# A two-model kernel on one core: shared banks for the output product, rope partners by DMA, a norm by pairs of tiles, and more convolution taps per portion

## The chip, the core and the metric

The program runs on one core of one Trainium2 chip. The metric is the time of one execution in microseconds (us), taken on the device. The five engines are called by their short names: PE multiplies matrices (PEld is its loading of weights), DVE is the vector engine, ACT the scalar engine, POOL the third element-wise engine, and SP the one that issues most transfers. Each engine works through its own list of instructions in a fixed order; only transfers and semaphores couple the lists.

## The reference, cut to what matters

Two models run one after the other on 256 tokens of width 1024, two layers each. The change is in the first one. One layer of it is:

```
n  = rmsnorm(h);  z = n @ w_in + b_in            # 1024 -> all branches
ya = conv(val * sigmoid(glu)) ...  * silu(c_gate)   # 31 taps, 256 channels
yb = pool_mixer(p_in)              * silu(p_gate)   # 256 channels
q, k = rope(q), rope(k);  index scores -> top 64 keys per query
yc = attention(q, k, v, only the chosen keys) * silu(a_gate)   # 512 channels
h  = h + concat(ya, yb, yc) @ w_out
h  = h + (p @ ple_w) * sigmoid(h @ ple_gate_w)
```

Rope turns each half of a head's 64 channels with its partner half: `x1*cos - x2*sin, x2*cos + x1*sin`. With the channels on the partitions the partner sits 16 partitions away in a group of 32 (the host orders the channels so).

## The kernel before, in words

All products keep nearly full float32 precision by splitting each operand into a high part and a low rest. A weight unit `raw` (128x1024) comes by DMA from SP; ACT copies it to the high part of `hl` (line 441) and DVE subtracts to get the low part (line 449). Each product is three matmuls (lines 388 to 390): high by high, high by low of the moving side, and low by high. Only the third needs DVE's half. There are four buffers for `raw` and four for `hl`, three PSUM banks "mm" for such products, four banks "ax" for the attention and the small products, and one bank "ada" for the second model's modulation product, whose pieces fill gaps of PE.

In program order a layer of the first model is: the norm (`norm`, lines 758 to 764), the value and gate of the convolution, the index keys and queries, the pool input, then four tiles of `q` and four of `k` (lines 839 to 848), each a product of 24 matmuls, closed by `rope` (lines 715 to 729); then `v` in four units, 48 wide matmuls (512 columns); eight gate tiles (lines 876 to 889); the output product (called the WO stage here, lines 895 to 908); and the per-token product of the last step. `rope` works on a pair of tiles at a time: a STREAM_SHUFFLE puts the partner halves into `ropes` (line 724), two multiplications and an addition of 512 columns follow (lines 727 to 729).

The WO stage multiplies the concatenated `xx` (eight chunks of 128 channels) in two halves g of four chunks, in the order WO_ORDER, so that the half g=0 can run while the last chunks are still computed. Each half makes eight tiles of 256 columns in an "mm" bank of its own, and each tile is added to `h` at once (line 903): sixteen additions a layer.

Four pieces run beside that as generators: `conv1` (31 taps on two tiles, line 945 on; each tap two SCALAR_TENSOR_TENSOR `acc<-u,sp,acc`), `index1` (the search for the 64th largest score by rounds of MAX8, line 1049, and MATCH_REPLACE8, line 1050), `pool1`, and `attn1`. A call of `tick` (line 460 on) after a tile hands the generators a budget; each runs until its next `yield n`, and n is taken off. `conv1` yields CONVY=900 after each tap, a gate tile hands out 1500. The instructions so written are then put in order on each engine by a scheduler with its own costs, except where `pin` keeps program order; so how the lists come out is read from the built program, not from the source. `until` and `flush` (lines 892 to 897) empty the generators where the WO stage needs their results; the tail of `conv1` (a layer norm over the channels: sums by `c,csq`, a row statistic on POOL `clr`, a spread, a tanh, the product with `sw`) and the tail of `attn1` (`aPT`, `yc`) produce the last chunks of `xx`.

## Time and profile before

| what | value |
|---|---|
| median of three timed runs | 1444.32 us (1443.57 to 1445.23) |
| the profiled execution | 1440.44 us, span of the trace 1438.6 us |
| mean granted TensorE clock | 0.98 of 2.4 GHz |
| the first model | about 0 to 377 us of the span; layer 1 starts near 207 us |
| WO stage, g=0 ends / g=1 goes on | 143.4 / 155.8 us (layer 0), 323.0 / 336.6 us (layer 1) |

The profiled execution is 3.9 us under the median; sums are made in its time. Busy times in the profile are shares of a stretch. Where both PE and DVE are busy for nearly the whole of a stretch, work that is put on either is paid in full; where both wait, a chain of single steps sets the time. A matmul's own duration overlaps with its neighbours' (they are pipelined); what one costs in a row is the distance between two starts, called its step, and the same holds for DVE.

### The profile page before, as it was taken

The numbers are of one execution on the slowest core, as the hardware profiler recorded it, in microseconds if no ns is written. First come the engines' busy times: TensorE is split into PE (matmuls) and PEld (weight loads), VectorE is DVE, ScalarE is ACT, GpSimd is POOL, SyncE is SP. The second block draws the span as 40 slices with busy tenths as digits, with TensorE's granted clock in tenths as the row PEclk, the third lists the DMA queues.
The fourth block names the chain that finished last, engine by engine and source line by source line (L and its number), as shares of the span: only waits on it lengthen the run. The fifth ranks groups of instructions, "written<-read, shape, count | busy, mean of one in ns | idle before, by whom it ended". The sixth has DMA issues, their size and how long they took to land.

```text
span 1438.6 us, 25329 instructions
## 1 busy us (share of the span) xinstructions
PE 1385.0 (96%) x9914; PEld 1185.0 (82%) x9914; DVE 1137.7 (79%) x2430; ACT 671.8 (47%) x1234; POOL 64.6 (4%) x92
## 2 busy tenths in 40 slices
PE   8999899998999999998899999999999999999997
PEld 7878899787978777777788888887888887999997
DVE  6998679997889776888999985888377556798694
ACT  4446465465754241545344322443255346565562
POOL 0000000000200001002000000000200000100001
PEclk9999899998999997999999999999999999999999
DMA  7974356433653330542544555567232332376662
GB/s 253 332 249 128 99 163 206 128 95 131 195 181 100 131 114 31 161 130 73 178 151 139 168 184 177 198 211 234 88 116 89 90 100 87 116 213 196 183 199 76
DMA packets 63903, 219.03 MB, mean 152 GB/s; under 512 B 7270, under 2 KB 12328, under 8 KB 63528
## 3 DMA queue, kind: packets, MB, share of 16 engines
q1 hardware_dynamic: 58368, 209.22, 45.3%
q10 hardware_dynamic: 5416, 8.20, 1.8%
q8 instruction: 78, 1.28, 0.4%
q14 instruction: 41, 0.34, 0.1%
HBM read 216.34 MB, written 1.05 MB: 151 GB/s over the span
## 4 chain that ended last, share of the span: by engine, by line
PE 70%; DVE 14%; issue 6%; DMA 4%; ACT 3%; POOL 1%; ACTq 0%; POOLq 0%; DVEq 0%; SPq 0%
PE mm L388 20%; PE mm L389 19%; PE mm L390 19%; PE ax L385 8%; DVE hl L449 3%; DMA wada<-in_wadaT_dram 3%; PE mm L385 2%; DVE wada L682 1%; PE ax L1725 1%; PE ada L385 1%; DVE ada L678 1%; DVE y L396 1%; ACT hl L441 1%; DMA raw<-in_units_dram 1%; DMA crow<-in_crow_dram 1%
## 5 line engine op out<-in xcount | busy, mean ns | idle before, releaser
L388 PE MATMUL mm<-xx,hl 128*128 128x256 f32 (+1 forms) x1720 | 557.0, 326 | 7.8 <-DVE x L396 2.3
L390 PE MATMUL mm<-xx,hl 128*128 128x256 f32 (+1 forms) x1720 | 547.2, 319 | 5.6 <-DVE hl L449 5.5
L389 PE MATMUL mm<-xx,hl 128*128 128x256 f32 (+1 forms) x1720 | 548.0, 319 | 0.2 <-DVE xx L396 0.2
L449 DVE TENSOR_TENSOR hl<-raw,hl 128x1024 fp32r<-128x1024 f32 x286 | 350.0, 1225 | 72.9 <-ACT hl L441 71.3
L441 ACT ACTIVATE hl<-raw 128x1024 fp32r<-128x1024 f32 x286 | 301.6, 1055 | 182.7 <-PE mm L390 144.4
L388 PEld LDWEIGHTS mm<-xx,hl 128*128 128x128 f32 x1720 | 325.5, 190 | 56.1 <-issue 18.1
L390 PEld LDWEIGHTS mm<-xx,hl 128*128 128x128 f32 x1720 | 325.8, 190 | 35.2 <-DVE hl L449 7.7
L389 PEld LDWEIGHTS mm<-xx,hl 128*128 128x128 f32 x1720 | 326.1, 190 | 29.0 <-issue 5.8
L388 PE MATMUL mm<-hid,hl 128*128 128x256 f32 (+1 forms) x374 | 123.0, 329 | 0.1
L389 PE MATMUL mm<-hid,hl 128*128 128x256 f32 (+1 forms) x374 | 122.9, 329 | 0.0
L390 PE MATMUL mm<-hid,hl 128*128 128x256 f32 (+1 forms) x374 | 122.5, 328 | 0.0
L396 DVE SCALAR_TENSOR_TENSOR y<-mm,sp,y 128x255 f32<-128x255 f32 (+1 forms) x184 | 108.6, 595 | 17.5 <-ACT y L409 16.3
L409 ACT ACTIVATE y<-mm,sp 128x256 f32<-128x256 f32 (+1 forms) x92 | 60.5, 658 | 105.7 <-PE mm L390 105.5
L682 DVE CUSTOM_DVE_ANT_0 wada<-wada,crow,sp 128x1024 f32<-128x1024 f32 x80 | 101.9, 1281 | 4.9 <-DMA wada<-in_wadaT_dram 4.3
L388 PEld LDWEIGHTS mm<-hid,hl 128*128 128x128 f32 x374 | 70.4, 188 | 7.7 <-ACT hid L414 0.5
L389 PEld LDWEIGHTS mm<-hid,hl 128*128 128x128 f32 x374 | 70.4, 188 | 7.4 <-DVE hid L415 0.4
L390 PEld LDWEIGHTS mm<-hid,hl 128*128 128x128 f32 x374 | 70.4, 188 | 6.9
L396 DVE SCALAR_TENSOR_TENSOR x<-mm,mod,x 128x256 f32<-128x256 f32 x96 | 43.9, 480 | 36.2 <-PE mm L390 36.0
L389 PE MATMUL mm<-hl,xx 128*128 128x416 f32 (+3 forms) x192 | 66.0, 346 | 2.5 <-DVE hl L449 2.5
L388 PE MATMUL mm<-hl,xx 128*128 128x416 f32 (+3 forms) x192 | 65.8, 348 | 0.2 <-ACT hl L441 0.2
L390 PE MATMUL mm<-hl,xx 128*128 128x416 f32 (+3 forms) x192 | 65.6, 343 | 0.0
L537 POOL TENSOR_TENSOR sqa<-sqa,sq 128x256 f32<-128x256 f32 x36 | 33.9, 946 | 677.5 <-ACT sq L409 676.9
(278 smaller groups left out, 1688.2 us busy)
## 6 DMA issues: line engine op xcount, KB each, us to landing
raw<-in_units_dram SPq DMA_DIRECT2D x296, 512.0 KB, 3.8
wada<-in_wadaT_dram SPq DMA_DIRECT2D x80, 512.0 KB, 4.6
wada<-in_wada_dram SPq DMA_DIRECT2D x16, 512.0 KB, 6.2
nab<-in_nab_dram ACTq DMA_DIRECT2D x12, 192.0 KB, 2.6
crow<-in_crow_dram SPq DMA_DIRECT2D x2, 1024.0 KB, 6.6
x<-in_xT_dram SPq DMA_DIRECT2D x4, 256.0 KB, 5.6
x<-in_ctxT_dram ACTq DMA_DIRECT2D x1, 1024.0 KB, 8.8
c<-in_c_dram ACTq DMA_DIRECT2D x1, 928.0 KB
```

The costliest lines, as they stand in the source:

```text
L385: return s.nc.tensor.matmul(out, lhsT, rhs, start=start, stop=stop, **kw)
L388: s.nc.tensor.matmul(out, l[0], r[0], start=start, stop=False)
L389: s.nc.tensor.matmul(out, l[0], r[1], start=False, stop=False)
L390: s.nc.tensor.matmul(out, l[1], r[0], start=False, stop=stop)
L396: s.nc.vector.scalar_tensor_tensor(out, a, sc, b, op0, op1)
L409: s.nc.scalar.activation(out, in_, func, bias=bias, scale=scale)
L441: a = nc.scalar.activation(hl[:, 0], raw, AF.Copy)
L449: b = nc.vector.tensor_sub(hl[:, 1], raw, hl[:, 0].bitcast(F32))
L537: (eng or s.nc.vector).tensor_tensor(st["acc"], st["acc"], sq, ALU.add)
L678: nc.vector.tensor_tensor_reduce(out=out, in0=w[:, c_], in1=c[:, j, c_], scale=1.0, scalar=b, op0=ALU.mult, op1=ALU.add, accum_out=mod[:, ...
L682: nc.vector.tensor_tensor_reduce(out=w, in0=w, in1=c[:, j], scale=1.0, scalar=bias[:, m : m + 1], op0=ALU.mult, op1=ALU.add, accum_out=mod ...
L1725: nc.tensor.transpose(pt[:, kt * 128 : kt * 128 + 128], L[j][:, kt * 128 : kt * 128 + 128], s.ident)
```

## The change

The diff, complete but for blank lines:

```diff
--- before.py
+++ after.py
@@ -23,7 +23,8 @@
 FIRST = 2
 PAIR_PACE = 2.0
 DOWN_PACE = 2.5
-CONVY = 900
+CONVY = 1300
+GATE_TICK = 2800
 INNER = 650
 INNER_K = (1, 3, 5)
 R_TICK, NQ_TICK, SC_TICK = 650, 900, 1000
@@ -563,6 +564,18 @@
         return ps
 
 
+    def part(s, out, hl, ks, off, g):
+        for q, k in enumerate(ks):
+            o = (q + off) * 128
+
+            s_, e_ = not g and not off and q == 0, bool(g) and bool(off) and q == len(ks) - 1
+            r = [s.mv(e, k, 0, T) for e in range(2)]
+            kw = dict(skip_group_check=True)
+            s.mm(out, hl[:, 0, o : o + 128], r[0], s_, False, **kw)
+            s.mm(out, hl[:, 0, o : o + 128], r[1], False, False, **kw)
+            s.mm(out, hl[:, 1, o : o + 128], r[0], False, e_, **kw)
+
+
     def ftile(s, x, keep=False):
         w = s.raw0.pop(0) if s.raw0 else s.rawunit()
         ps = s.bank("mm")
@@ -712,16 +725,23 @@
         s.pin(s.nc.gpsimd.tensor_tensor(r, ms[:, 0:4], s.mhalf[:, :4], ALU.pow))
         return r[:, 0:2], r[:, 2:4]
 
-    def rope(s, raw, n, eng=None):
+    def rope(s, raw, n, eng=None, swap=False):
 
         tt = (eng or s.nc.vector).tensor_tensor
         if n > 2:
             for a in range(0, n, 2):
-                s.rope(raw[:, a : a + 2], 2, eng)
+                s.rope(raw[:, a : a + 2], 2, eng, swap)
             return
         sh = s.t([128, 2, T], "ropes", ROPEB)
         f = lambda x: x.rearrange("p a t -> p (a t)")
-        s.nc.vector.stream_shuffle(f(sh[:, :n]), f(raw), SHUF)
+        if swap:
+
+            hv = lambda x: x.rearrange("(g h r) a t -> g h r a t", h=2, r=16)
+            for e in range(2):
+                for g in range(4):
+                    s.pin(s.nc.scalar.dma_start(hv(sh[:, :n])[g, e], hv(raw)[g, 1 - e]))
+        else:
+            s.nc.vector.stream_shuffle(f(sh[:, :n]), f(raw), SHUF)
         cb = s.cos.unsqueeze(1).to_broadcast([128, n, T])
         sb = s.sin.unsqueeze(1).to_broadcast([128, n, T])
         tt(raw, raw, cb, ALU.mult)
@@ -758,10 +778,10 @@
         def norm():
             R = s.spread(s.rstd_cols(s.st[0]["ps"][:, 0:2], 2, 1.0 / D), 2)
             s.a(rs, R[:, :T], AF.Copy)
-            for k in range(KT):
-                n = s.t([128, T], "nf", 2, pool=s.sm)
-                s.tt(n, gh[:, k], rs, ALU.mult)
-                s.split(s.xx[:, 1, 0, k], s.xx[:, 1, 1, k], n)
+            for k in range(0, KT, 2):
+                n = s.t([128, 2, T], "nh", 2)
+                s.tt(n, gh[:, k : k + 2], rs.unsqueeze(1).to_broadcast([128, 2, T]), ALU.mult)
+                s.split(s.xx[:, 1, 0, k : k + 2], s.xx[:, 1, 1, k : k + 2], n)
 
         tile_no = [-1]
         raws = [s.ftile(gh, i == 0 and j == 0) for j in range(FIRST)]
@@ -844,7 +864,7 @@
                 ps = wtile()
                 s.a(raw[:, j], ps[:, :T], AF.Identity, bias=bias()[0])
                 s.tick()
-            s.rope(raw, 4)
+            s.rope(raw, 4, swap=True)
             qk.append(raw)
 
         s.pool_share = SHARE[1]
@@ -886,25 +906,29 @@
             if i == DEPTH - 1 and j == RCTX:
                 ps = s.spread(rc, 2)
                 s.a(s.rctx, ps[:, :T], AF.Copy)
-            s.tick()
+            s.tick(GATE_TICK)
         s.pace = PACE[3]
         s.pool_share = 0.0
         s.until(st8, "pool")
         s.until(st8, ("att", 1))
 
 
+
+        wo = [s.bank("mm" if b < 3 else "ada") for b in range(4)]
         for g in range(2):
             if g:
                 s.turns = False
                 s.flush()
-            for m in range(KT):
-                if m % 2 == 0:
-                    hl = s.unit()
-                ps = s.mtile(0, T, hl, WO_ORDER[4 * g : 4 * g + 4], m % 2 * 4)
-                s.tt(h[:, m], h[:, m], ps[:, :T], ALU.add)
+            for m in range(0, KT, 2):
+                hl, ps = s.unit(), wo[m // 2]
+                for d in range(2):
+                    s.part(ps[:, d * T : d * T + T], hl, WO_ORDER[4 * g : 4 * g + 4], d * 4, g)
+                    if not g:
+                        s.tick()
                 if g:
-                    s.split(s.xx[:, 1, 0, m], s.xx[:, 1, 1, m], h[:, m])
-                s.tick()
+                    hm = h[:, m : m + 2]
+                    s.tt(hm, hm, ps.rearrange("p (k t) -> p k t", k=2), ALU.add)
+                    s.split(s.xx[:, 1, 0, m : m + 2], s.xx[:, 1, 1, m : m + 2], hm)
         s.pace = PACE[4]
         if i < DEPTH - 1:
             s.spn = s.small1(i + 1)
@@ -956,7 +980,8 @@
             for j in range(2):
                 s.stt(acc[:, j], u[:, j, k : k + T], P["dw"][:, j * CONV_K + k : j * CONV_K + k + 1], acc[:, j],
                       ALU.mult, ALU.add)
-            yield CONVY
+            if k % 2 == 0:
+                yield CONVY
         while "late" not in st8:
             yield None
         o256 = s.t([128, 128], "o256", 1)
```

Of this the last hunk makes `conv1` yield 1300 after every second tap; a gate tile now hands out 2800. `part` runs half a tile's chunks into a bank that stays open: the four shared banks `wo` each hold two tiles of 256 columns, g=0 starts the accumulation in them, g=1 adds onto it, and only then one addition and one split follow for each pair of tiles. The generators get a turn only in g=0. `rope` for `q` and `k` fetches the partner halves with eight transfers of 16 partitions x 512 columns (32 KB) for each pair of tiles, issued by ACT in program order: 16 after the fourth `q` tile, 16 after the fourth `k` tile, 32 a layer. The norm forms and splits 512 columns at a time. The number of matmuls stays as it was, POOL's list is the same, and SP's changes in three rows.

How the lists of instructions move, at three places of layer 0. DVE between the low halves of the third and the fourth `k` tile; before, the low half hl_712 serves the third and hl_765 the fourth (names end in a running number that differs between the two builds):

```order
L449 TENSOR_TENSOR hl_712<-raw_710,hl_712 128x1024
L396 SCALAR_TENSOR_TENSOR isc_535<-irl_553,pin_290,isc_535 128x128
L724 STREAM_SHUFFLE ropes_608<-qr_437 128x512
L1049 MAX im_557<-isc_535 128x8
L727 TENSOR_TENSOR qr_437<-qr_437,c_101 128x512
L1050 MATCH_REPLACE iwk_556<-im_557,isc_535 128x128
L728 TENSOR_TENSOR ropes_608<-ropes_608,c_101 128x512
L1049 MAX im_557<-iwk_556 128x8
L729 TENSOR_TENSOR qr_437<-qr_437,ropes_608 128x512
L1050 MATCH_REPLACE iwk_556<-im_557,iwk_556 128x128
L449 TENSOR_TENSOR hl_765<-raw_763,hl_765 128x1024
```

and now, the last rows ahead of the fourth tile's low half, which is called hl_771 (the third's, hl_718, stands 45 rows above it):

```order
L397 SCALAR_TENSOR_TENSOR acc_374<-u_190,sp_80,acc_374 128x256
L406 TENSOR_TENSOR imk_702<-iwk_548,isc_527 128x128
L397 SCALAR_TENSOR_TENSOR acc_374<-u_190,sp_80,acc_374 128x256
L403 TENSOR_SCALAR imk_702<-imk_702 128x128
L397 SCALAR_TENSOR_TENSOR acc_374<-u_190,sp_80,acc_374 128x256 x4
L397 SCALAR_TENSOR_TENSOR isc_705<-irl_708,pin_274,c_101 128x256
L747 TENSOR_TENSOR qr_429<-qr_429,c_101 128x512
L748 TENSOR_TENSOR ropes_607<-ropes_607,c_101 128x512
L397 SCALAR_TENSOR_TENSOR isc_705<-irl_713,pin_274,isc_705 128x256
L749 TENSOR_TENSOR qr_429<-qr_429,ropes_607 128x512
L397 SCALAR_TENSOR_TENSOR isc_705<-irl_755,pin_274,isc_705 128x256
L450 TENSOR_TENSOR hl_771<-raw_769,hl_771 128x1024
```

The fourth low half moved behind 20 taps (`acc<-u,sp,acc`), eight MAX8 and eight MATCH_REPLACE8, six rope steps of 512 columns and three index sums; before, no tap, two MAX8 and two MATCH_REPLACE8, one index sum and three rope steps with their shuffle stood between the two. In layer 1 it is the same with 23 taps. All 62 tap instructions of a layer now come ahead of the first gate tile; before, 24 did.

PE at the end of the WO stage's first half; before, from the sums of the convolution's layer norm to the second half's first tiles, which go on there (mm_1716 and so on):

```order
L385 MATMUL ax_1662<-c_82,csq_1660 128x1 x4
L385 MATMUL ax_1671<-c_82,clr_1669 128x128 x2
L385 MATMUL ax_1684<-csq_1660,sw_102 128x256
L385 MATMUL ax_1690<-csq_1660,sw_102 128x256
L1102 MATMUL ax_1696<-c_82,aL_1593 128x128
L385 MATMUL ax_1684<-csq_1660,sw_102 128x256
L385 MATMUL ax_1690<-csq_1660,sw_102 128x256
L1102 MATMUL ax_1696<-c_82,aL_1593 128x128 x3
L385 MATMUL ax_1624<-aPT_1701,v_816 64x128 x4
L388 MATMUL mm_1716<-xx,hl_1713 128x256
L388 MATMUL mm_1732<-xx,hl_1713 128x256
L388 MATMUL mm_1753<-xx,hl_1750 128x256
```

and now, from the last rows of attention (`aPT`, `aL`) among the products of the open banks (mm_1562, mm_1563, mm_1564, ada_1565) to the second half (mm_1562 again, with hl_1713):

```order
L386 MATMUL mm_1562<-xx,hl_1568 128x256 x4
L386 MATMUL ax_1588<-aPT_1586,v_836 64x128 x2
L386 MATMUL mm_1562<-xx,hl_1568 128x256 x7
L1127 MATMUL ax_1597<-c_82,aL_1557 128x128 x2
L386 MATMUL mm_1562<-xx,hl_1568 128x256
L1127 MATMUL ax_1597<-c_82,aL_1557 128x128 x2
L386 MATMUL mm_1563<-xx,hl_1626 128x256 x12
L386 MATMUL ax_1588<-aPT_1602,v_836 64x128 x4
L386 MATMUL mm_1563<-xx,hl_1626 128x256 x12
L386 MATMUL mm_1564<-xx,hl_1655 128x256 x24
L386 MATMUL ada_1565<-xx,hl_1684 128x256 x24
L386 MATMUL mm_1562<-xx,hl_1713 128x256 x24
```

The convolution's small products (`c,csq`, `c,clr`, `csq,sw`) left this place and stand further up, and 60 matmuls of the first half now follow the last product of attention (ax_1588 with aPT_1602), where none did.

ACT around the fourth `q` tile; before:

```order
L441 ACTIVATE hl_712<-raw_710 128x1024
L409 ACTIVATE irl_553<-ax_551 128x128
L409 ACTIVATE qr_437<-mm_565,sp_80 128x256
L441 ACTIVATE hl_765<-raw_763 128x1024
L409 ACTIVATE kr_613<-mm_619,sp_80 128x256
L441 ACTIVATE hl_821<-raw_819 128x1024
L409 ACTIVATE kr_613<-mm_662,sp_80 128x256
L441 ACTIVATE hl_852<-raw_850 128x1024
```

and now:

```order
L442 ACTIVATE hl_718<-raw_716 128x1024
L410 ACTIVATE irl_545<-ax_543 128x128
L410 ACTIVATE qr_429<-mm_557,sp_80 128x256
L742 DMA ropes_595<-qr_429 16x512 x8
L742 DMA ropes_607<-qr_429 16x512 x8
L410 ACTIVATE kr_619<-mm_625,sp_80 128x256
L410 ACTIVATE kr_619<-mm_668,sp_80 128x256
L410 ACTIVATE irl_708<-ax_706 128x256
L410 ACTIVATE irl_713<-ax_711 128x256
L410 ACTIVATE kr_619<-mm_721,sp_80 128x256
L442 ACTIVATE hl_771<-raw_769 128x1024
```

Sixteen DMA issues stand between the last `q` tile's bias step and the first `k` tile's, and the high half of the fourth `k` tile (hl_771) comes later among its neighbours.

## Rows read from the trace of the kernel before

**Rows 1.** The page's busy times over the whole span.

```profile
PE 1385.0 (96%) x9914; PEld 1185.0 (82%) x9914; DVE 1137.7 (79%) x2430; ACT 671.8 (47%) x1234; POOL 64.6 (4%) x92
```

**Rows 2.** Stretches of layer 0: length, busy PE, PEld, DVE, ACT, POOL, clock, DMA, GB/s.

```profile
44.00:64.00 20.00, 20.00 (x181) 16.69 (x183) 19.85 (x41) 9.33 (x16) 0.00 (x0) 1.00 0.94 328
64.00:84.00 20.00, 20.00 (x144) 14.17 (x144) 19.78 (x57) 9.82 (x16) 0.00 (x0) 1.00 0.92 313
...
143.00:156.00 13.00, 7.59 (x38) 5.80 (x38) 6.41 (x17) 4.33 (x9) 0.70 (x1) 0.73 0.13 41
```

**Rows 3.** The same view, stretches of layer 1.

```profile
250.00:270.00 20.00, 18.21 (x93) 13.45 (x92) 20.00 (x60) 6.03 (x8) 1.20 (x1) 1.00 0.24 79
270.00:290.00 20.00, 18.69 (x145) 16.31 (x146) 17.37 (x43) 12.62 (x32) 0.41 (x1) 1.00 0.51 159
...
320.00:337.00 17.00, 9.67 (x44) 7.05 (x44) 12.03 (x24) 5.20 (x10) 1.61 (x1) 0.79 0.39 125
```

**Rows 4.** Timeline of PE, layer 0, end of g=0: start, length, count, idle before.

```profile
146.10 1.22 PE L385 MATMUL ax<-c,clr 128*128 128x128 f32 x4 [1.03 <-POOL clr L519]
149.50 2.08 PE L385 MATMUL ax<-csq,sw 128*128 128x256 f32 x4 [2.17 <-DVE csq L396]
...
155.76 0.93 PE L388 MATMUL mm<-xx,hl 128*128 128x256 f32 x3 [0.98 <-ACT xx L414]
156.49 0.41 PE L389 MATMUL mm<-xx,hl 128*128 128x256 f32 x1
```

**Rows 5.** Timeline of PE, layer 1, the same place.

```profile
323.81 1.05 PE L385 MATMUL ax<-c,csq 128*128 128x1 f32 x8 [0.82 <-ACT csq L409]
...
326.81 1.22 PE L385 MATMUL ax<-c,clr 128*128 128x128 f32 x4 [1.72 <-POOL clr L519]
330.41 3.44 PE L385 MATMUL ax<-csq,sw 128*128 128x256 f32 x8 [2.38 <-DVE csq L396]
...
336.60 0.88 PE L388 MATMUL mm<-xx,hl 128*128 128x256 f32 x3 [0.97 <-ACT xx L414]
```

**Rows 6.** Timeline of DVE, layer 0, third and fourth k tile.

```profile
58.19 1.22 DVE L449 TENSOR_TENSOR hl<-raw,hl 128x1024 fp32r<-128x1024 f32 x1
...
61.88 0.29 DVE L1049 MAX8 im<-iwk 128x8 f32<-128x128 f32 x1
62.08 0.67 DVE L729 TENSOR_TENSOR qr<-qr,ropes 128x512 f32<-128x512 f32 x1
62.67 0.08 DVE L1050 MATCH_VALUE_LOAD iwk<-im,iwk 128x8 f32 x1
62.74 0.28 DVE L1050 MATCH_REPLACE8 iwk<-im,iwk 128x128 f32<-128x128 f32 x1
62.94 1.22 DVE L449 TENSOR_TENSOR hl<-raw,hl 128x1024 fp32r<-128x1024 f32 x1
```

**Rows 7.** Timeline of DVE, eight taps in a row.

```profile
37.98 3.26 DVE L396 SCALAR_TENSOR_TENSOR acc<-u,sp,acc 128x256 f32<-128x256 f32 x8
```

**Rows 8.** Timeline of PE, layer 0, ada group ahead of the fourth k tile.

```profile
68.09 0.64 PE L385 MATMUL ada<-wada,cs 128*32 128x256 f32 x8
...
69.29 0.38 PE L388 MATMUL mm<-xx,hl 128*128 128x256 f32 x1
```

**Rows 9.** Timeline of PE, layer 1, waits for DVE in v and gates.

```profile
259.79 0.51 PE L389 MATMUL mm<-hl,xx 128*128 128x512 f32 x1 [0.79 <-DVE hl L449]
...
280.53 0.39 PE L390 MATMUL mm<-xx,hl 128*128 128x256 f32 x1 [1.31 <-DVE hl L449]
```

**Rows 10.** DVE groups by shape, 28 to 88 us: count, busy us, mean ns.

```profile
L724 DVE STREAM_SHUFFLE ropes<-kr 128x512 f32<-128x512 f32 x2 | 1.5, 742 | 0.0
...
L727 DVE TENSOR_TENSOR ki<-ki,c 128x256 f32<-128x256 f32 x1 | 0.4, 426 | 0.0
```

**Rows 11.** A DMA issued by ACT (line 800): ns of issue, us to landing.

```profile
L800 ACTq DMA_DIRECT2D tokb<-in_tokb_dram x2: 334/334/334, 24.6 to 207.8; - x2
...
DMA to landing us min/median/max: 6.0/6.9/7.8
```

## The prediction, made before the changed kernel ran

> **What bounds the kernel now.** I read the page first, then the stretches by engine, then PE's timeline where the stretches show it waiting, then DVE's. PE is busy for 1385.0 us of 1438.6 [rows 1], so anything to be gained lies in the places where it isn't. In layer 0 of the first model there is one such place: from 143 to 156 us PE is busy for 7.59 us of 13, at a granted clock of 0.73 [rows 2]; in layer 1 the same place takes 17 us with 9.67 busy at 0.79 [rows 3]. The timeline names the chain: the convolution's layer norm, statistic by statistic (POOL `clr`, then DVE `csq`), then the end of attention, then ACT's last split of `xx` [rows 4, 5]. Elsewhere in these layers PE runs without a gap, 20.00 of 20 us from 44 to 84, and there DVE is as full, 19.85 and 19.78 of 20 [rows 2]. So the front of the layer is tight on two engines at once and the back is a chain of single steps. The change takes work out of the back and puts work into the front; the forecast is the difference of the two.
>
> **What the tail gives back.** In layer 0 PE's last product before the chain ends near 143.4 and the second half goes on at 155.76 [rows 4], 12.4 us later. About 32 matmuls lie in between; at the step of 0.113 us that back-to-back products have at full clock they are worth 3.6, so 8.8 are lost. After 155.76 the products are 0.41 us long instead of 0.28 [rows 4], the half clock, with a step of 0.213; it lasts until about 159.2, 16 matmuls by 0.10 us, 1.6 more. Together 10.4. In layer 1: from 323.0, the end of the last product that ran freely, to 336.60 [rows 5] are 13.6 us, 33 matmuls in them worth 3.7, so 9.9; with the half clock again 1.6, together 11.5. The changed list of PE has the small products of the layer norm further up and 60 products of open banks behind attention's last product, 60 by 0.113 = 6.8 us, against the chain from `aPT` to `xx` of about 2 us (the waits of 0.98 and 0.97 are its last step [rows 4, 5]). So the whole of both tails should go. I keep back 1 us a layer for attention's own chain, which now ends with less other work around it: 10.4 + 11.5 - 2 = 19.9 us gained.
>
> **What the taps cost in front.** All 62 tap instructions now precede the first gate tile, where 24 did, and a tap's step is 3.26 / 8 = 0.41 us [rows 7]: 38 by 0.41 = 15.6 us of DVE work put into a stretch where DVE has 0.2 us in 20 to spare. Four shuffles leave it, 742 ns each [rows 10]. Both ends: if everything stands in front of what PE waits for, PE loses 15.6 - 4 x 0.63 = 13 us a layer; if PE's third products never wait for it, nothing. The order decides. Between the third and the fourth `k` tile's low halves DVE had 4.75 us of work (58.19 to 62.94 [rows 6]). Now it has 20 taps (8.2), eight MAX8 at 0.20 and eight MATCH_REPLACE8 at 0.27 with their loads (3.8), six rope steps of 512 columns at 0.59 (3.5), three index sums and two mask steps (1.6), and the split itself (1.13, all steps from [rows 6]), 18 to 19 us. Summing DVE's steps from the start, the fourth low half is ready at about 76.9 us. PE began this tile at 69.29, after an ada group that takes 0.57 to the next start [rows 8]; with three more such groups moved ahead and the products that only need the high half, it comes to the third product at about 71.3. It waits 5.6 us. For the last `v` unit the same sum gives 95.2 against 93.2, 2.0 us, and for the first gate 0.5: together 8.1 in layer 0.
>
> In layer 1 there are 23 taps and six index sums in the same place; the low half is ready at about 258.2 and PE is there at about 250: 8.2 us. The rope of `k` follows later than its index products want it (2.6), the last `v` unit 1.2: 12.0. From this goes what PE waits there already, since DVE is then further ahead: 0.79 and 1.31 are single waits [rows 9], and PE is busy for 18.21 and 18.69 of 20 us [rows 3], 3.1 in sum; by the few matmuls in these 40 us it is nearer 5. I take 4, so 8.0.
>
> A wait of such a length can also lower the clock, which costs about 1.6 as above. In layer 0 the next wait (2.0) would take it up, since DVE's times don't move with PE's; in layer 1 the next ones (3.8) too. It is left out of the sum for that reason.
>
> The Trainium skill ("TensorE: Matmul & The Clock Gate", What's actually happening) says that PE falls back to half its rate after an idle stretch; the half-clock products behind both tails agree. By that rule the new waits in `k` are paid for once more if nothing behind them takes it up; that is the fourth rival below.
>
> **The small parts.** The norm goes from eight steps of 256 columns to four of 512. A 256-wide multiplication takes 426 ns [rows 10], a 512-wide one 0.67 us [rows 6], so a pair saves 0.2; with multiplication and split that is up to 1.5 us a layer on DVE, some of it beside ACT's halves. PE waits for the first pair longer and for the last less. Between 0 and -1.5 I take -0.6 a layer. The sixteen additions of the WO stage become four of 512 columns; before, PE's products hid them, and now the last pair's addition and split stand between the last product and the next stage, which starts with a product that doesn't need them: nothing, at most +0.5.
>
> The swap of rope partners: 16 issues stand in ACT's list after `q` and 16 after `k`. A DMA issue on ACT takes 334 ns here and the transfer lands 6.0 to 7.8 us later [rows 11] (those were larger transfers into a loaded system; the DMA share from 64 to 84 us is 0.92 [rows 2], so I take them as they are). Sixteen issues hold ACT for 5.3 us at least, but ACT is busy for only 9.33 of 20 [rows 2]. The issues begin when `q`'s last tile is out, at about 57.7; the first pair's eight are out at about 60.4 and landed at 66 to 68. DVE gets to the first pair's addition at about 67.1. So the transfers are on the edge, the second pair less so, as it is wanted later. I take 0 for the swap, and keep as bounds -2.5 a layer (the shuffles' time) and +6 (four waits of about 3 us over both layers, in the rival below).
>
> The Trainium skill ("DMA: Bandwidth & Descriptors", Anatomy of one DMA) gives a fixed cost of about 2.0 us for each DMA; this trace has 6.9 in the median [rows 11]. By the page the swap would never be late and the sum would stay as it is; the measurement decides.
>
> **Sum.** Layer 0: +8.1 - 0.6 - 10.4 + 1 = -1.9. Layer 1: +8.0 - 0.6 - 11.5 + 1 = -3.1. Together -5.0, from 1440.44 of the profiled execution to 1435.4; that execution is 3.9 under the median of the runs, so in the median's frame 1439.3.
>
> **The rivals.**
>
> *The front pays it all back.* DVE is the bound from the fourth `k` tile to the gates, and every tap moved is paid for, 13 us a layer, less 4 us of waits that layer 1 has already, less the tails: 26 - 4 - 19.9 - 1.2 = +0.9, so 1445. For it: DVE at 19.8 of 20 [rows 2]. Against it: the order puts some other DVE work behind the point where PE waits.
>
> *The swap holds DVE (slower).* The additions of a pair wait in DVE's fixed list for eight transfers that land together with the weight stream, and all splits behind them wait too. If the first pair lands 3 us after DVE asks, at four places, that is +12: 1451. It decides from a landing of about 7 us after the last issue on; the median in [rows 11] lies just there, the longest above. Against it: the transfers are only 32 KB.
>
> *The taps are hidden (much faster).* If PE's products in the front find their low halves ready in time because the scheduler's order has slack that my sum doesn't see, the 16 us in front are not paid: 1423. Against it: no stretch of DVE from 44 to 84 with room.
>
> *The clock falls in the new waits.* +1.6 a layer: 1442.5.
>
> **How the numbers follow.** Likeliest 0.40, 1439.3, its own range 1433 to 1444; front pays back 0.17; swap slower 0.18; hidden 0.14; clock 0.11. A difference under 0.2% (2.9 us) can't be told from none here: faster is under 1441.4. Faster takes 0.34 of the likeliest, 0.14 and 0.03 of the last and 0.02 of the wash, 0.53; slower takes the swap's 0.18 and 0.03 of the wash, 0.21; the rest, 0.26, is the same. The range runs from 1426, where most of the hidden case is left out, to 1450, where half of the swap's case is.
>
> **What would show it.** Right: no idle PE stretch at the end of the WO stage's first half in either layer, and a single wait of about 6 (layer 0) and 8 us (layer 1) before the third product of the fourth `k` tile, put down to DVE `hl`. PE would go from the first to the second half of layer 0's WO stage near 155.5 us (143.4 + 8.1 - 0.6 + 3.6 + 1) at full clock, without a break. Wrong: waits of DVE at line 749 or 748 for `ropes` over 1 us (the swap), a PE without waits between 65 and 100 (hidden), products of 0.41 us in `v` or the gates with no wait behind them (clock), or an idle stretch that remains before the second half.

## The result: slower by half a per cent, and the profile after

The median went from 1444.14 us (1443.57 to 1446.89, six runs) to 1452.67 us (1450.24 to 1457.84, six runs); the ratio is 1.0054, 95% interval 1.0035 to 1.0074. The profiled execution took 1450.24 us, span 1448.5, clock 0.977. The forecast was 1439.3, with a range from 1426 to 1450: the kernel became slower, not faster.

Four marks on PE's timeline split the two layers into front and back: the first product of attention with `v` (aPT) and the first product after the WO stage (qi,hl), in layer 0 and layer 1. Before (start, length, what):

```profile
102.67 0.44 PE L385 MATMUL ax<-aPT,v 128*64 128x128 f32 x4
...
167.35 0.28 PE L388 MATMUL ax<-qi,hl 128*128 128x256 f32 x1
...
281.20 0.44 PE L385 MATMUL ax<-aPT,v 128*64 128x128 f32 x4
...
348.49 0.28 PE L388 MATMUL ax<-qi,hl 128*128 128x256 f32 x1
```

and after:

```profile
116.38 0.44 PE L386 MATMUL ax<-aPT,v 128*64 128x128 f32 x4
...
173.72 0.28 PE L389 MATMUL ax<-qi,hl 128*128 128x256 f32 x1
...
297.57 0.44 PE L386 MATMUL ax<-aPT,v 128*64 128x128 f32 x4
...
355.38 0.28 PE L389 MATMUL ax<-qi,hl 128*128 128x256 f32 x1
```

| part | measured | forecast |
|---|---|---|
| front of layer 0, to 116.38 | +13.7 | +7.5 |
| back of layer 0, to 173.72 | -7.3 | -9.4 |
| front of layer 1, to 297.57 | +10.0 | +7.4 |
| back of layer 1, to 355.38 | -9.5 | -10.5 |
| sum | +6.9 | -5.0 |

(13.7 is 116.38 - 102.67, -7.3 is 6.37 - 13.71, and so on; the forecast's norm stands in the fronts, its 1 us for attention in the backs.) By these marks the fronts cost 23.7 us instead of 14.9, and the backs gave 16.8 instead of 19.9. The mark `aPT` is not at the same place of PE's list in the two kernels, though: of the gates' products of 256 columns, 18 in layer 0 and 24 in layer 1 that stood ahead of it before stand behind it now. At their step of 0.113 us these are 2.0 and 2.7 us of work that left the fronts, so with equal work the fronts cost about 28.4 us and the backs gave about 21.6. The miss lies in the fronts alone.

The stretches of after, as in [rows 2, 3]:

```profile
64.00:84.00 20.00, 15.07 (x113) 9.98 (x112) 19.86 (x53) 7.36 (x14) 0.00 (x0) 0.83 0.58 175
84.00:104.00 20.00, 15.34 (x90) 10.14 (x89) 14.43 (x44) 4.29 (x9) 0.15 (x1) 0.84 0.76 240
143.00:156.00 13.00, 12.90 (x101) 10.49 (x100) 9.69 (x29) 7.99 (x22) 0.00 (x0) 1.00 0.27 81
250.00:270.00 20.00, 11.82 (x63) 9.86 (x64) 19.60 (x52) 6.71 (x12) 0.70 (x1) 0.70 0.21 51
270.00:290.00 20.00, 18.50 (x75) 13.88 (x74) 18.40 (x51) 5.67 (x11) 0.00 (x0) 0.79 0.46 144
320.00:337.00 17.00, 16.96 (x131) 14.08 (x131) 13.53 (x40) 12.51 (x31) 0.00 (x0) 1.00 0.31 94
```

The tails are closed: PE is busy for 12.90 of 13 and 16.96 of 17 us where [rows 2, 3] had 7.59 and 9.67, and although the second half now begins 7 to 8 us later, from 116 to 180 us PE is busy for 63.68 of 64 and from 300 to 360 for 59.85 of 60. But from 64 to 104 us, where PE had no gap before ([rows 2], and for the second stretch

```profile
84.00:104.00 20.00, 20.00 (x165) 15.61 (x164) 19.93 (x54) 10.23 (x26) 0.00 (x0) 1.00 0.73 253
```

in the same view), it is busy for only 15.07 and 15.34 of 20, at a clock of 0.83 and 0.84, and from 250 to 270 us for 11.82 at 0.70.

The end of the WO stage's first half on PE's timeline of after:

```profile
155.35 0.66 PE L386 MATMUL ax<-aPT,v 128*64 128x128 f32 x8
155.94 4.35 PE L386 MATMUL mm<-xx,hl 128*128 128x256 f32 x36
160.12 2.88 PE L386 MATMUL ada<-xx,hl 128*128 128x256 f32 x24
162.84 5.38 PE L386 MATMUL mm<-xx,hl 128*128 128x256 f32 x46
```

The last product of attention (155.35) is followed by 60 products of open banks (36 + 24), and the second half goes on at 162.84 without a wait, where [rows 4] had three. The front, on PE's timeline:

```profile
70.08 0.64 PE L386 MATMUL ada<-wada,cs 128*32 128x256 f32 x8
...
75.23 0.58 PE L389 MATMUL mm<-xx,hl 128*128 128x256 f32 x1 [4.50 <-ACT hl L442]
...
80.30 0.48 PE L391 MATMUL mm<-xx,hl 128*128 128x256 f32 x1
...
98.17 0.80 PE L386 MATMUL ax<-kr,qr 64*128 64x128 f32 x4 [4.34 <-DVE kr L749]
```

and on ACT's (ACTq is its queue of issues):

```profile
57.85 0.60 ACTq L742 DMA_DIRECT2D ropes<-qr  x1
57.99 0.48 ACT L410 ACTIVATE qr<-mm,sp 128x256 f32<-128x256 f32 x1
58.49 13.94 ACTq L742 DMA_DIRECT2D ropes<-qr  x15
72.48 0.84 ACT L410 ACTIVATE kr<-mm,sp 128x256 f32<-128x256 f32 x2 [14.01 <-DMA ropes<-qr]
...
74.09 1.08 ACT L442 ACTIVATE hl<-raw 128x1024 fp32r<-128x1024 f32 x1
...
83.20 0.48 ACT L410 ACTIVATE kr<-mm,sp 128x256 f32<-128x256 f32 x1 [3.84 <-PE mm L391]
83.26 14.72 ACTq L742 DMA_DIRECT2D ropes<-kr  x16
98.03 1.06 ACT L442 ACTIVATE hl<-raw 128x1024 fp32r<-128x1024 f32 x1 [14.35 <-DMA ropes<-kr]
```

PE stops at about 70.7 for 4.50 us, named to ACT's `hl`. ACT was not computing: around the last `q` tile (57.99) stand 16 issues in one row, 15 of them in 13.94 us, and only then the biases of `k` and the high half of the fourth `k` tile (74.09). The same after `k`: 16 issues, 14.72 us. In layer 1 the two rows take 11.77 and 10.93 us, and PE waits there too:

```profile
257.58 0.62 PE L386 MATMUL ax<-c,sqa 128*128 128x1 f32 x4 [3.39 <-ACT irl L410]
...
262.60 0.58 PE L389 MATMUL mm<-xx,hl 128*128 128x256 f32 x1 [3.54 <-ACT hl L442]
...
280.62 0.49 PE L386 MATMUL ax<-kr,qr 64*128 64x128 f32 x4 [1.50 <-DVE kr L749]
```

The first of these waits ends with what stood behind ACT's row of `q`; the second follows 3.05 us in which ACT itself waited for DVE. From the source line's own view, issue in ns (min/median/max) and us to landing:

```profile
L742 ACTq DMA_DIRECT2D ropes<-qr x32: 514/600/1057, 57.9 to 255.8; - x32
L742 ACTq DMA_DIRECT2D ropes<-kr x32: 513/600/602, 83.3 to 281.3; - x32
...
DMA to landing us min/median/max: 1.9/3.9/6.4
```

One issue takes 600 ns; with the pauses between them they start 0.92 us apart in layer 0 and 0.7 in layer 1. The row I had priced them by showed 334 [rows 11]. DVE's timeline shows the rest of it:

```profile
77.05 1.22 DVE L450 TENSOR_TENSOR hl<-raw,hl 128x1024 fp32r<-128x1024 f32 x1
...
95.90 0.69 DVE L747 TENSOR_TENSOR kr<-kr,c 128x512 f32<-128x512 f32 x1 [5.53 <-DMA wada<-in_wada_dram]
```

At 77.05 DVE starts the fourth tile's low half (the forecast had it ready at 76.9; it is ready at 78.2), and before 95.90 it idles 5.53 us ahead of the first rope step of `k`. The view puts the release down to a `wada` load, which has nothing to do with `kr`. The time fits the swap: the first pair's eight issues begin at 83.26, the last of them at 90.82, and its own row says

```profile
L742 ACTq DMA_DIRECT2D ropes<-kr x1: 602/602/602, 90.8 to 90.8; - x1
...
DMA to landing us min/median/max: 4.8/4.8/4.8
```

so it landed at 95.62. Rope's first step (line 747) overwrites `kr`, which the transfers read, and so can't begin before they are done. PE then waits 4.34 us for `kr` (98.17 above).

### The profile page after: what moved, and what is told of

Its sections match the earlier page's. It is cut to its first block, busy times and chain, and to the rows that moved or that the text cites. A ratio compares the mean times of both kernels' runs of the same rounds, so it can differ in the third digit from the quotient of the medians.

```text
span 1448.5 us, 25348 instructions
## 1 busy us (share of the span) xinstructions
PE 1387.9 (96%) x9914; PEld 1187.1 (82%) x9914; DVE 1126.5 (78%) x2366; ACT 666.9 (46%) x1218; POOL 62.4 (4%) x92
## 4 chain that ended last, share of the span: by engine, by line
PE 74%; DVE 12%; DMA 6%; ACT 4%; issue 3%; POOL 1%; ACTq 0%; POOLq 0%; DVEq 0%; SPq 0%
PE mm L389 19%; PE mm L391 19%; PE mm L390 19%; PE ax L386 9%; PE mm L386 5%; DVE hl L450 3%; DMA wada<-in_wadaT_dram 2%; PE ada L386 1%; ACT hl L442 1%; DVE wada L695 1%; DMA raw<-in_units_dram 1%; DVE ada L691 1%; PE ax L1750 1%; DVE y L397 1%; DMA ropes<-qr 1%
## 5 line engine op out<-in xcount | busy, mean ns | idle before, releaser
L389 PE MATMUL mm<-xx,hl 128*128 128x256 f32 (+1 forms) x1592 | 522.3, 329 | 15.4 <-ACT hl L442 10.7
L391 PE MATMUL mm<-xx,hl 128*128 128x256 f32 (+1 forms) x1592 | 512.5, 323 | 5.2 <-DVE hl L450 5.1
L390 PE MATMUL mm<-xx,hl 128*128 128x256 f32 (+1 forms) x1592 | 512.6, 323 | 0.5 <-DVE xx L397 0.2
L389 PEld LDWEIGHTS mm<-xx,hl 128*128 128x128 f32 x1592 | 302.5, 190 | 61.5 <-issue 17.7
L391 PEld LDWEIGHTS mm<-xx,hl 128*128 128x128 f32 x1592 | 301.6, 190 | 35.8 <-DVE hl L450 7.4
L390 PEld LDWEIGHTS mm<-xx,hl 128*128 128x128 f32 x1592 | 302.1, 190 | 28.3 <-issue 4.6
L389 PE MATMUL mm<-hl,xx 128*128 128x416 f32 (+3 forms) x192 | 67.7, 360 | 0.9 <-ACT hl L442 0.9
L390 PE MATMUL mm<-hl,xx 128*128 128x416 f32 (+3 forms) x192 | 67.0, 351 | 0.5 <-DVE hl L450 0.5
L391 PE MATMUL mm<-hl,xx 128*128 128x416 f32 (+3 forms) x192 | 66.5, 348 | 0.0
```

The source lines that it names most:

```text
L389: s.nc.tensor.matmul(out, l[0], r[0], start=start, stop=False)
L390: s.nc.tensor.matmul(out, l[0], r[1], start=False, stop=False)
L391: s.nc.tensor.matmul(out, l[1], r[0], start=False, stop=stop)
```

## The experiments

Theory S: the cost is the swap, whose issues hold ACT, and the rest of the change is a gain. Theory F, my forecast's: the cost is the taps that come earlier. Ratios are to the kernel before, run on the same chip; the chips differ from run to run, so runs are compared by their ratios. "The planner" is the scheduler that puts each engine's list in order. The edits are cut to the lines that matter.

| run | what it is | median us | ratio (95% interval) |
|---|---|---|---|
| changed kernel | all parts | 1452.67 | 1.0054 (1.0035 to 1.0074) |
| e1_no_swap | all but the swap | 1435.01 | 0.9930 (0.9906 to 0.9953) |
| e2_swap_alone | before + swap | 1471.61 | 1.0199 (1.0168 to 1.0231) |
| e3_swap_on_sp | changed, SP issues | 1450.99 | 1.0045 (1.0019 to 1.0072) |
| e4_swap_by_fours | changed, 8 x 64 KB | 1450.79 | 1.0051 (1.0030 to 1.0071) |
| e5_banks_alone | before + banks | 1440.58 | 0.9967 (0.9950 to 0.9985) |
| e7_pacing_alone | before + pacing | 1436.94 | 0.9932 (0.9909 to 0.9954) |
| e10_swap_unread | e1 + transfers nobody reads | 1445.10 | 0.9992 (0.9980 to 1.0005) |
| e11_unread_quarter | e10, 8 KB each | 1449.65 | 1.0042 (1.0023 to 1.0061) |
| e12_swap_on_pool | changed, POOL issues | 1437.72 | 0.9943 (0.9923 to 0.9962) |
| e8_old_taps_new_gates | e1, old tap pace | 1434.33 | 0.9922 (0.9908 to 0.9936) |
| e13_pool_old_taps | e12, old tap pace | 1425.01 | 0.9867 (0.9844 to 0.9891) |

**Without the swap.**

```diff
-            s.rope(raw, 4, swap=True)
+            s.rope(raw, 4)
```

> The changed kernel with the shuffles back in place of the swap transfers; all else stays. Theory S (the swap is the cost: 16 issues of about 0.9 us hold ACT for 14 us after q and after k, so the high halves of the weights come late, and the planner, which sees that, fills DVE with taps meanwhile): the front waits of 4.5 and 4.3 us in layer 0 and 3.4, 3.5 and 1.5 us in layer 1 and their half clock go, the tails stay closed; from about 1450 by 18 to 24 us down, 1424 to 1432. Theory F (DVE has no room for the earlier taps wherever they stand, here in the gates): the gain of the tails is paid back in the gates, 1437 to 1445, with waits of PE for DVE's low halves between 87 and 125 us.

Measured: 0.9930, some 10 us under before and 18 under the changed kernel. The list of DVE of this kernel settles where the taps came from: with the shuffles back, 21 taps stand ahead of the fourth `k` tile's low half in layer 0, as before, instead of 48. It wasn't the pacing that brought them to this place; the planner did, once the swap's issues stood in ACT's list. That it did so because it saw ACT held is my reading. Theory S's direction holds, its size does not: 1435 lies above its 1424 to 1432. Stretches of this kernel:

```profile
64.00:84.00 20.00, 19.98 (x142) 14.02 (x141) 20.00 (x62) 8.44 (x14) 0.00 (x0) 1.00 0.89 311
84.00:104.00 20.00, 19.35 (x153) 14.18 (x153) 18.56 (x50) 8.68 (x22) 0.00 (x0) 1.00 0.38 128
250.00:270.00 20.00, 13.98 (x52) 9.84 (x51) 19.04 (x47) 3.55 (x4) 0.93 (x1) 0.83 0.25 79
```

The front of layer 0 is whole again (19.98 and 19.35), but in layer 1 PE idles for 6 us between 250 and 270 (1.8 before [rows 3]), at a clock of 0.83, in waits like those of [rows 9], longer now:

```profile
257.61 0.51 PE L390 MATMUL mm<-hl,xx 128*128 128x512 f32 x1 [1.46 <-DVE hl L450]
...
263.56 0.79 PE L390 MATMUL mm<-hl,xx 128*128 128x512 f32 x1 [2.91 <-DVE hl L450]
```

These are low halves of the third and fourth unit of `v`: with two taps for each yield, 20 and 28 taps of the layer stand ahead of them, where 12 and 16 did.

**The swap alone.**

```diff
-            s.rope(raw, 4)
+            s.rope(raw, 4, swap=True)     # with the changed rope(), in the kernel before
```

> The kernel before with nothing but the swap transfers in place of the shuffles. Theory S: the front waits appear as in the changed kernel (PE idle 4 to 5 us near 71 and near 94), and the taps come forward with them, 48 ahead of the v units, though no tap pacing was changed; part of the tail goes too because the taps are done earlier. Slower than before by 3 to 12 us, 1447 to 1456. Theory F: the swap alone does little, within 3 us of 1444, since it takes 2.5 us of shuffles a layer off DVE.

Measured 1.0199, 27 us by the medians and far over the 12 us allowed. The front cost appears as said, and 48 taps stand ahead of the fourth tile again. But nothing comes back behind it; PE's timeline at the tail of layer 0:

```profile
161.66 0.71 PE L385 MATMUL ax<-c,clr 128*128 128x128 f32 x4 [1.03 <-POOL clr L519]
164.54 2.08 PE L385 MATMUL ax<-csq,sw 128*128 128x256 f32 x4 [2.17 <-DVE csq L396]
...
170.83 0.85 PE L388 MATMUL mm<-xx,hl 128*128 128x256 f32 x3 [0.98 <-ACT xx L414]
```

These are the waits of [rows 4], to 0.01 us. All taps are long done (by 100 us), and the layer norm's chain still waits for its turn in the program: when `conv1` goes on after the taps is the pacing's doing, as e7 below bears out.

**Who issues.**

```diff
-                    s.pin(s.nc.scalar.dma_start(hv(sh[:, :n])[g, e], hv(raw)[g, 1 - e]))
+                    s.pin(s.nc.sync.dma_start(hv(sh[:, :n])[g, e], hv(raw)[g, 1 - e]))      # e3
+                    s.pin(s.nc.gpsimd.dma_start(hv(sh[:, :n])[g, e], hv(raw)[g, 1 - e]))    # e12
```

> The changed kernel with the swap transfers issued by SP instead of ACT, pinned as there. If what costs is that ACT's queue is held (issue theory), ACT's high halves are no longer late and PE's waits near 71 and 94 shrink to those for DVE's low halves; but SP's own weight loads then wait behind the issues, so a wait for raw may take their place: 1438 to 1450. If what costs is the late landing of the partner halves (landing theory), DVE still idles about 5 us near k's rope and the time stays at 1450 to 1456.

1.0045: between the two expectations, and undecided by time. SP's weight loads came behind the issues, of which one waited 7.5 us for `kr` in SP's queue, and DVE's list had 37 taps even ahead of the third `k` tile.

> The changed kernel with the swap transfers issued by POOL, whose list is nearly empty, instead of ACT. Nothing of ACT or SP is held; DVE still waits for the partner halves to land. Hold theory (what costs is the held queue and what it delays): near the kernel without the swap, 1434 to 1441. Landing theory (the transfers land late whoever issues them): DVE idles several us ahead of the rope additions and PE's waits near 71 and 94 us stay, 1445 to 1453.

0.9943, 16 us under the changed kernel (0.0111 of 1444), and not told apart from e1. These are the same transfers, issued by an engine with little else to do, and they land no sooner:

```profile
L742 POOL DMA_DIRECT2D ropes<-qr x32: 484/484/707, 49.3 to 236.1; - x32
...
DMA to landing us min/median/max: 1.7/5.5/7.1
```

The median of 5.5 us is longer than the 3.9 of the changed kernel, and PE has no wait over 0.4 us between 40 and 250 us (this execution, 1428.06 us, was the shortest of nine). So a late landing by itself is not what costs; the held queue is. In the changed kernel a landing still ends waits, DVE's of 5.53 us above and pauses of ACT's row below; but there the issues had left late. Here POOL begins those of `k` at 64.17 instead of 83.26, the first pair has landed by 74.61, and rope's first step starts at 75.18 without a wait for it.

**Issues without use.**

```diff
-                    s.pin(s.nc.scalar.dma_start(hv(sh[:, :n])[g, e], hv(raw)[g, 1 - e]))
-        else:
-            s.nc.vector.stream_shuffle(f(sh[:, :n]), f(raw), SHUF)
+                    s.pin(s.nc.scalar.dma_start(hv(du)[g, e], hv(s.c1v)[g, 1 - e]))
+        s.nc.vector.stream_shuffle(f(sh[:, :n]), f(raw), SHUF)
```

> The changed kernel without the swap in its arithmetic (shuffles are back), but with the same 64 transfers issued by ACT at the same places, from a constant tile into a tile that nobody reads. Nothing waits for their landing. If the cost of the swap is the hold of ACT's queue (issue theory, 14 us after q and after k, with the taps that the planner moves in front of the low halves), PE waits near 71 us as in the changed kernel and the time is 1445 to 1453. If it is DVE's wait for the landed partners (landing theory), the time is near that of the kernel without the swap, 1435 to 1440.

0.9992, 9 us over the kernel without the swap: at the lower edge of the issue theory. On ACT and on PE in layer 0:

```profile
58.26 15.56 ACTq L744 DMA_DIRECT2D dummy<-c  x16
```

```profile
76.62 0.58 PE L389 MATMUL mm<-xx,hl 128*128 128x256 f32 x1 [5.49 <-ACT hl L442]
```

So holding ACT, with the taps that come forward with it (39 ahead of the fourth tile), cost about 9 us here although nobody reads what is moved. The other 9 of the swap's 18 I put down to the use: `k`'s partners are issued one behind the other, so its rope, and attention, are late, and PE's waits for `kr` (4.34 and 1.50) are gone in this kernel. That split is argued, from kernels whose lists differ; no run holds ACT without moving taps, and in e11 below a shorter hold cost more than 9 us.

**Price of an issue.** e4: eight transfers of four tiles (`sh = s.t([128, 4, T], "ropes", 1)`); e11: `[..., :64]` on both sides of the unread transfers.

> The changed kernel with the partner halves of all four q (or k) tiles fetched by eight transfers of 64 KB instead of sixteen of 32 KB. If each issue has a price of its own (0.9 us whatever its size), ACT is held 7.5 us instead of 14 after q and after k, the wait for the high half near 71 us shrinks to less than 1 us but DVE's work in front of the low half keeps PE waiting there; 1444 to 1449. If the price goes with bytes or rows moved, ACT is still held 14 us and the time stays at 1450 to 1457.

> The kernel with the unread transfers, each with a quarter of the columns (8 KB instead of 32 KB), issued by ACT at the same places. If an issue has one price whatever it moves (0.9 us), ACT is held about 14 us and the time is that of the unread transfers, 1443 to 1447. If the price has a part by bytes, as 1.37 us for 64 KB and 0.93 us for 32 KB suggest (0.44 us per 32 KB), an issue costs about 0.6 us, ACT is held about 10 us and the time is 1437 to 1442.

Eight issues of 64 KB held ACT for 10.99 us after `q` in layer 0, sixteen of 8 KB for 12.45; with 32 KB it was 14.58, and 15.56 unread. The price goes neither by issue alone nor by bytes alone, because such a row has two parts. The issues take nearly the same whatever they move: 4.5 us for the eight (0.56 each), 9.6 for sixteen of 32 KB (0.60), 10.7 for sixteen of 8 KB (0.67). The rest, 6.5, 5.0 and 1.7 us, are pauses between them, and by the semaphores in the traces most of their time is a wait for an earlier transfer to land, of the swap or of the weights. In the changed kernel the seventh issue after `k` starts at 90.24, and the transfer issued at 83.81 landed at 90.22.

Time followed neither expectation: e4 is as slow as the changed kernel, e11 by its ratio 16 us slower than e1 and some 7 slower than e10, although ACT was held less. In e11 the planner placed fewer taps forward (30 ahead of the fourth tile against 39), and PE waits at another place instead:

```profile
92.15 1.94 PE L386 MATMUL ada<-wada,cs 128*32 128x256 f32 x16 [4.45 <-ACT adae L410]
```

There ACT's step `adae`, which PE's `ada` products wait for, stands behind the 16 issues of `k` (it starts at 91.71); in the changed kernel and in e10 it stands ahead of them, at 76.51 and 77.9. So what stands behind the row matters beside its length.

**The other parts alone.**

```diff
+        wo = [s.bank("mm" if b < 3 else "ada") for b in range(4)]      # e5: with part() and the new WO loop
-CONVY = 900
+CONVY = 1300     # e7: with every second yield, and s.tick(2800) in the gate loop
```

> The kernel before with nothing but the output product in four shared banks (one addition and split for each pair of tiles). DVE's list up to the gates is that of before. If the tail was closed by the banks, PE's idle places near 146 to 156 and 324 to 337 us go and the time falls by 15 to 20 us. If it is the tap pacing and the larger budget of a gate tile that bring the convolution's layer norm forward (pacing theory), its chain still stands between the halves here and only the second half's restart may change: within 4 us of before, 1441 to 1447.

> The kernel before with nothing but CONVY=1300 after every second tap and 2800 for a gate tile. Pacing theory: the sums c,csq and clr are made in the first half of the output product, POOL's and DVE's waits of 1.0 and 2.2 us (1.7 and 2.4 in layer 1) go, the end of attention stays as a chain of 2 us: 8 to 14 us faster than before, 1430 to 1437, about as the changed kernel without the swap. If the banks are what closes the tail: within 4 us of before.

Banks 0.9967, pacing 0.9932. With banks alone PE's waits for `clr` (0.81) and `csq` (2.17) stand; with pacing alone there is no idle place from 136 to 165 us. The pacing closes the tail, as it was expected to; the banks gain 5 us, somewhat over the 4 allowed. Together, and with the norm (e1), they are no better than the pacing: 0.9930.

**Better versions.** e8 is e1 with `CONVY = 900` after each tap; e13 is e8 with the swap issued by POOL.

> The changed kernel without the swap and with the old pace of the taps (CONVY=900 after each), only the gate tile's budget of 2800 and the banks and the norm kept. Up to v the taps stand as before (12 in layer 1 instead of 16), so the waits of 1.5 and 2.9 us in v of layer 1 that the kernel without the swap showed should shrink to about 0.8; the layer norm's chain comes a unit later. If the chain still ends in time: 1430 to 1436, as good as or better than without the swap; if not, 1437 to 1442 with the idle places near 146 us back in part.

> The changed kernel with the swap transfers issued by POOL and with the old pace of the taps (CONVY=900 after each), so that what is left of the change is the banks, the gate tile's budget, the norm by pairs and the swap on an engine that has time for it. If the two gains add (the swap on POOL takes 2.5 us of shuffles a layer off DVE, the old pace keeps four taps out of the front of layer 1), the time is 1428 to 1434, below the 1434.3 of the version with shuffles. If DVE is no longer what PE waits for, or the transfers land late, it is the same within 3 us: 1432 to 1438.

e8 came out in its range, 0.9922, not told apart from e1; the waits in layer 1's `v` fell to one of 1.18 us. e13 is the fastest of all, 0.9867, 18 us under before, better than expected. Against e8 the swap on POOL gains about 8 us there (0.0055 of 1444), more than the 5 us of shuffles that it takes off DVE; at the new tap pace, e12 against e1, it gained nothing that shows. Where the rest of the 8 us comes from was not followed up.

## Why the prediction was wrong, step by step

**The tail.** Right in place and in what PE's list does there: 16.8 us by the marks, 21.6 with equal work, where 19.9 were forecast. Which edit does it the forecast left open; e7 shows that the pacing closes the tail, e5 that the banks alone don't.

**The taps in front.** The place was right, the fourth `k` tile, with PE there at 70.7 (forecast 71.3) and the low half ready at 78.2 (76.9). The wait was not: I had said a single one of about 6 us before the third product, for DVE's low half; what came is 4.50 us before the first product, for ACT's high half. The reason was wrong too. I charged the 38 taps to the pacing; e1, e2 and e7 show that the 20 in front of the fourth tile are moved by the swap. Ahead of the first gate tile stand 24 taps before, 38 with the pacing alone (e7) and all 62 with the swap alone (e2). I had both lists before me, and the ACT list with its sixteen issues, and did not ask which edit moved which row.

**The swap, the step that failed.** "Sixteen issues hold ACT for 5.3 us at least", and "I take 0". The 334 ns came from one DMA of another shape [rows 11]; measured are 600 ns an issue, and with the waits for earlier landings between them 14.6 us for sixteen in layer 0 and 11 to 12 in layer 1. ACT's busy share (9.33 of 20 [rows 2]) was taken for room, but the issues are one block in a fixed list, and behind it stood the high half that PE wanted next. The swap with the taps that it moves costs 18 us (e1 against the changed kernel) or 27 (e2 against before), where my sum had 16.1 for the taps and 0 for the swap. With equal work the fronts cost about 13.5 us more than forecast, with DVE idle for 5.53 us and PE for 4.34 ahead of `kr` in layer 0 alone. How much of this is ACT's hold and how much the moved taps, no run separates.

The landings were taken for longer than they are: 6.0 to 7.8 us in the forecast, 1.9 to 6.4 measured, 3.9 in the median. (The 2.0 us that the prediction takes from the Trainium skill, "DMA: Bandwidth & Descriptors", Anatomy of one DMA, are given there for a DMA that GpSimd (POOL here) issues, which the prediction doesn't say; its sum does not use them.) The rival "the swap holds DVE" had the sign and 1451, with a late landing at four places as its cause. At one of them DVE did wait for a landing, the 5.53 us above; at the other three it waited for less than 0.5 us, and e12, with longer landings, is as fast as the kernel without the swap.

**The clock.** I let the next wait take up the half clock. In layer 0 the granted clock was 0.83 and 0.84 in the two stretches from 64 to 104, and the half level behind both waits:

```profile
75.20:80.00 4.80, 4.35 (x22) 1.94 (x22) 4.80 (x8) 4.16 (x7) 0.00 (x0) 0.50 0.12 21
...
98.20:104.00 5.80, 5.80 (x27) 3.83 (x28) 5.76 (x18) 4.12 (x9) 0.15 (x1) 0.50 0.73 193
```

At it 18 `ada` products took 2.77 us, where eight take 0.64 ahead of the wait, and 12 products `c,pin` 2.80 us, where 12 more take 1.66 at full clock later. So each of the two waits cost at least the rival's 1.6 us once more, and it was not taken up: behind the first wait PE reached the third product at 80.30, when its low half had been ready for 2 us, and behind the second the next wait over 0.4 us is one of 0.47 at 108.41.

**The small parts.** The norm: from the statistics' first product (`ax<-c,sqa`, 14.90 us before) to the first product of the pool input (28.43) PE's timeline has 13.53 us before, 13.52 with the old norm in e5 and e7, and 13.14, 13.24 and 13.23 with the new one in the changed kernel, e1 and e8. So the norm by pairs gains 0.3 to 0.4 us there in layer 0, where I took 0.6; layer 1 was not read.

## What to carry to other kernels

Before a cheap-looking transfer replaces a vector instruction, price its issue on the engine that issues it, times their number in a row, add the landings that later issues of the row wait for, and look at what stands behind the row in that engine's list; a busy share says nothing of a block of 14 us. When an order is made by a planner, build each edit alone and compare the lists: which edit moved a row decides whose cost it is. Here an engine that had little to do was the place for such issues, although they landed later there.

## What the runs showed that was not expected

In the second model the changed kernel's lag, product by product, is 6.2 us from about 760 to 1200 us of the span before, and 9.8 at the end. PE's timelines near the second model's statistics, before:

```profile
1241.11 0.61 PE L385 MATMUL ax<-c,sqa 128*128 128x1 f32 x4 [1.57 <-POOL sqa L537]
...
1242.02 1.55 PE L385 MATMUL ada<-mhalf 128*128 128x256 f32 x6
```

and after:

```profile
1246.94 0.61 PE L386 MATMUL ax<-c,sqa 128*128 128x1 f32 x4 [1.72 <-POOL sqa L538]
...
1247.86 2.88 PE L386 MATMUL ada<-mhalf 128*128 128x256 f32 x6
```

PE waits 1.72 instead of 1.57 us, and the six `ada` products of the last row took 2.88 instead of 1.55: the granted clock of the surrounding 30 us is 0.94 against 1.00. The change doesn't touch this model, so some 3.6 us of the 9.8 between these two executions are put down to the clock here and not to the change. Runs of one kernel differ by such steps: the changed kernel's six runs stand at 1450.2 to 1450.7 with a mean clock of 0.977 to 0.978, and at 1454.7 to 1457.8 with 0.970 to 0.972. That each higher run is such a drop more was not tested.
